# Two strips of squares moved from the end of the first projection to behind the second step of the second one

## The chip, the core and the metric

The kernel runs on one core of a Trainium2 chip. Each core has a matrix engine (TensorE, in the profile PE, its weight loads PEld), a vector engine (VectorE, DVE), an engine for activations, casts and copies (ScalarE, ACT), a general engine (GpSimd, POOL) and one that issues loads (SyncE, SP). Each runs its own queue of instructions in order, and semaphores join them. Transfers between memory and the core's buffers go over 16 DMA engines that all queues share; in this kernel SP's queue issues the loads and ACT's queue the stores. The metric is the time of one execution on the device in microseconds, as the median of several runs.

## The reference

The reference is one layer of a hybrid block over 1024 positions of width 1024, all in float32. Cut to what matters:

```python
proj = h @ w_in                                   # h: normed x with scale and shift from c
gm_u, gm_v, gm_z, ssm_z, xbc, dt_raw, g_a, g_b = jnp.split(proj, SPLITS, axis=-1)
y_a = spatial_gating(gelu(gm_u), gelu(gm_v), ...) * silu(gm_z)
...
y_b = ssd_scan(xh, dt, a, bm, cm) + xh * d_skip[:, None]
yz = (y_b.reshape(b, s, 2048) * silu(ssm_z)).reshape(b, s, 8, 256)
y_b = rms_norm(yz, ssm_norm_w.reshape(8, -1)).reshape(b, s, 2048)
merged = sigmoid(g_a) * (y_a @ w_proj_a) + sigmoid(g_b) * (y_b @ w_proj_b)
return rms_norm(x + gate * (merged @ w_out), final_norm_w)
```

The change concerns `rms_norm(yz, ...)`: in each of the 8 groups a position's 256 values are divided by the root of their mean square. The sum of squares over 256 values lies across partitions in the kernel, so it is made on TensorE.

## The kernel before

The kernel holds activations transposed: the channel on the 128 partitions, the position in the free dimension, in halves of 512. A large product is computed with each float32 operand as a high part (rounded, type fp32r) and a low part (the rest), and three matmuls: high x high, high x low, low x high.

**Stages.** Norm and modulation; the product with `w_in`; the gMLP branch; then the state-space branch, 8 groups of 4 heads each, two groups at a time. Beside this branch runs the *first projection* (`y_a @ w_proj_a`, function `proj_a`): 8 blocks of 24 pairs of matmuls (`pma`), which `draw(n)` issues n pairs at a time to fill TensorE. At a block's end VectorE forms `tha` from the block's two banks (L1488) and ACT's queue stores it as `mt_d` (L1490). Behind it comes the *second projection* (`y_b @ w_proj_b`), in Strassen's form: seven products of half size, p1, p3, p6, p5, p7, p2, p4 in this order, each of eight steps k. One step of one product is called a unit here: `multiply` (L1676), 12 matmuls, into four banks `x0p` to `x3p` or `y0p` to `y3p`. p1 uses the x banks; the y banks are first written by p3, at unit 8. After it come the product with `w_out` and the last norm.

**Operands of a unit.** `loads(u)` runs 6 units ahead (LOAD): it issues on SP's queue the load `yn` of the unit's 128 channels from `yb_d`, for every second such load the factors `rb` (L91, `rs_d` of the group, the same for all partitions), and the weight, either a strip `p1r` of 256 KB or a ready pair of high and low part (`p3a`, 512 KB, from `wb_d`). `operands(u)` runs 4 units ahead (LEAD): VectorE normalises `yn` with `rb` (L1614), ScalarE casts the high half `bh` (L1651), VectorE forms the low half `bl` (L1652); for p1 the same two steps for the weight (L1656, L1657). Units 0 to 7 (p1) need the normalised channels of groups 0 to 3, units 8 to 15 (p3) those of groups 4 to 7; the first unit that needs group 6 is unit 12, group 7's is unit 14.

**The factors of a group.** `post` stores a half (512 positions) of `yz` to `yb_d`; the squares follow (ScalarE, L1246 or L1251, then POOL adds the two tiles of a group, L1247). `post2` makes the sums: four small matmuls with a strip of ones, one for each 128 positions, into four 32-row strips of one bank. This is the *strip of squares*, in the profile `pq<-yz,ones`. VectorE scales the bank into a constant's tile that is free by then, `cwt` for an even group and `tri` for an odd one (L1267), and ACT's queue stores it as `ms_d` (L1268). `post3` loads that as `ssq` (SP's queue, L91), `root` takes the power -1/2 on POOL (L1282), `post4` stores `rs_d` (ACT's queue, L94). For the second halves of the last two groups, 6 and 7, these steps are placed by hand: both strips among the last pairs of the first projection, `post3` and `root` behind unit 1, `post4` behind unit 4.

**What sets the order.** `pin` keeps an instruction where the program has it on its engine; all matmuls and all loads are pinned, the scalings and `ms_d` stores of these two strips too. What is not pinned is placed by the language's scheduler. For their completion the transfers of SP's and of ACT's queue take eight counters in turn (`DMAHW0` to `DMAHW7` in the order below), so each issue waits until the transfer eight places back, on whichever of the two queues, has landed.

Of the kernel before, what the change touches and what calls it, by code (L numbers as in the profile page):

```python
# [35 lines left out]
def hybrid_kernel(  # L36
# [1255 lines left out]
    groups = [Group(g) for g in range(NG)]  # L1292
    rows_bank = [bank]
# [222 lines left out]
    def draw(n):  # L1516
        for _ in range(n):
            left[0] -= next(fill, 1) is None
# [48 lines left out]
    def banks(name, c):  # L1567
        return [psb.tile([P, 512], F32, name=f"{name}{j}", tag=f"b{c}{j}") for j in range(4)]
# [52 lines left out]
    def loads(u):  # L1621

        nm, k = units[u]
        if nm in fresh:
            n, h = fresh[nm]
            y_load(n + k, h)
        aops[u] = t = big(f"{nm}a{k}", F32R).rearrange("p (v c) -> p v c", v=2)
        if nm in WB:
            load(f32(t), wb_d[k][:, WB[nm]])
        else:  # L1630
            raws[u] = raw = gate_slot(f"{nm}r{k}") if nm == "p1" else slot_tile(f"{nm}r{k}")
            n = k if nm == "p1" else KT + k
            load(raw, w_proj_b[n * P : (n + 1) * P, 0:512])
# [35 lines left out]
    def multiply(u, ps):  # L1669
        nm, k = units[u]  # L1670
        first = nm in ("p1", "p5", "p2", "p3")
        a, (bh, bl) = aops.pop(u), bops.pop(u)
        for j in range(4):
            js = slice(j * P, (j + 1) * P)
            for n, (v, r) in enumerate(((0, bh), (0, bl), (1, bh))):
                pin(PE.matmul(ps[j], a[:, v, js], r, start=first and n + k == 0, stop=n == 2 and k == KT - 1,  # L1676
                              skip_group_check=not first))
# [89 lines left out]
    def ahead(u):  # L1767
        if u + LOAD < len(units):
            loads(u + LOAD)
        if u + LEAD < len(units):  # L1770
            operands(u + LEAD)

    draw(left[0] - 8)
    groups[6].post2(1, groups[6].late[:1])
    for u in range(LOAD):
        loads(u)
        if u > 1:
            operands(u - 2)
        if u == 3:
            draw(left[0] - 3)  # L1780
            groups[7].post2(1, groups[7].late[:1])
    draw(left[0] + 1)
    room.extend(tag for k in (KT - 2, KT - 1) for tag in ya_tags[k])
    for tags, _ in (war_r[0], wah_r[0], wal_r[0], tha_r):
# [10 lines left out]
    for u, (nm, k) in enumerate(units):  # L1795
        if k == 0:
            if nm == "p1":
                first = {t: psb.tile([P, 512], F32, name=f"{t}p", tag=f"b{t}") for t in ('x0', 'x1', 'x2', 'y3', 'y0', 'y1', 'y2', 'x3')}
                psx, psy = ([first[f"{v}{j}"] for j in range(4)] for v in "xy")
            elif nm in ("p5", "p2"):  # L1800
                psy = banks(f"y{nm}", "y")
            ps = psy if nm in ("p2", "p5", "p3") else psx
        multiply(u, ps)
        ahead(u)
        if nm == "p1" and k == 2:
            for tags, _ in (y1_r, ym_r):
                room.extend(tags)
        if nm == "p1" and k in (1, 4):
            for late in groups[NG - 2 :]:
                late.post4() if k == 4 else late.post3()  # L1810
            if k == 1:
                for late in groups[NG - 2 :]:
                    late.root()
        if nm == "p2" and k == 4:
            room.extend(rb_r[0])
        if k % 2 and nm in GATES:
            gate_load(GATES[nm][0] + k // 2, GATES[nm][1])
        if nm == "p4":
            for at, f, a in BESIDE:
                if at == k:  # L1820
                    f(*a)
        if nm in ("p7", "p2", "p4") and k % 2 == (nm != "p4"):
            merged(*more.pop(0))
        if k == KT - 1:
            for j in range(4):
                with tc.high_priority():
                    if nm in ("p1", "p3", "p5"):
                        t = slot_tile(f"{nm}_{j}")
                        A.copy(t, (psx if nm == "p1" else psy)[j])
                        sums[nm, j] = t  # L1830
                    if nm == "p6":
                        V.tensor_add(sums["p3", j], sums["p3", j], psx[j])
                    elif nm == "p5":
                        V.tensor_add(sums["p3", j], sums["p3", j], sums["p5", j])
                        more.append((j, 1, sums["p3", j], f"p3_{j}"))
                    elif nm == "p7":
                        V.tensor_add(sums["p5", j], sums["p5", j], psx[j])
                        more.append((4 + j, 1, sums["p5", j], f"p5_{j}"))
                    elif nm == "p2":
                        V.tensor_add(sums["p1", j], sums["p1", j], psy[j])  # L1840
                        more.append((j, 0, sums["p1", j], f"p1_{j}"))
                    elif nm == "p4":
                        merged(4 + j, 0, None, None)
# [179 lines left out]
```

## Time and profile before

| what | value |
| --- | --- |
| median of 3 runs | 1369.64 us (1369.30 to 1369.72) |
| profiled execution | 1367.94 us, its span 1366.0 us |
| granted clock of TensorE in it | 0.999 |
| TensorE busy | 1352.3 us (99% of the span) |
| VectorE busy | 1045.9 us (77%) |
| ScalarE busy | 799.2 us (59%) |
| POOL busy | 192.5 us (14%) |
| strip of the second half of group 6 on TensorE | at 1124.37 us |
| the same of group 7 | at 1128.17 us |
| first matmul of the second projection | at 1130.02 us |

Times in the profile are microseconds from the start of the span. A row of a timeline gives an instruction's start, its length, engine, line, operation, and in brackets how long the engine had been idle before it and which engine or transfer ended that. A row with xN stands for several instructions in a run.

### The profile page before, as it was taken

To read this page: it belongs to the slowest core of one execution; us is meant where nothing else is said; L and a number is where in the kernel's file an instruction comes from. 1 tells how busy PE (TensorE), PEld (TensorE's weight loads), DVE (VectorE), ACT (ScalarE), POOL (GpSimd) and SP (SyncE) were. 2 spreads that over 40 slices of the span, in tenths; PEclk is the share of its full clock that TensorE was granted. 3 is DMA by queue.
4 is the path that set the end of the run, shared out by engine and by line. 5 is a ranking of instruction groups with operands and counts; after the bars stand their busy time and mean duration, and the time that the engine had idled before them with its cause. 6 is when DMAs were issued, how large, how long until landed. Compare 5 with 4: busy or idle time off the path is not lost.

```text
span 1366.0 us, 20176 instructions
## 1 busy us (share of the span) xinstructions
PE 1352.3 (99%) x6943; PEld 1116.6 (82%) x6943; DVE 1045.9 (77%) x1716; ACT 799.2 (59%) x1447; POOL 192.5 (14%) x191
## 2 busy tenths in 40 slices
PE   8999999999999999999999999999999999999997
PEld 7688888888888888888888888888888887888886
DVE  4786876777778888697887797458888866859976
ACT  5763666666666656466566556486877834233443
POOL 1000000000000000000000000006798971000002
PEclk9999999999999999999999999999999999999999
DMA  9674444334344657877656675589889959988903
GB/s 286 181 244 135 142 124 120 104 117 124 108 139 139 181 181 230 252 230 241 211 180 189 219 247 167 166 282 314 305 299 307 309 201 320 325 268 322 382 37 124
DMA packets 249530, 288.65 MB, mean 211 GB/s; under 512 B 16812, under 2 KB 196436, under 8 KB 249428
## 3 DMA queue, kind: packets, MB, share of 16 engines
q1 hardware_dynamic: 174868, 203.80, 46.9%
q10 hardware_dynamic: 74560, 83.57, 17.9%
q8 instruction: 55, 0.90, 0.3%
q14 instruction: 47, 0.39, 0.1%
HBM read 199.82 MB, written 87.49 MB: 210 GB/s over the span
## 4 chain that ended last, share of the span: by engine, by line
PE 92%; DMA 3%; DVE 2%; ACT 1%; SPq 1%; issue 0%; POOL 0%; POOLq 0%; DVEq 0%; ACTq 0%
PE xz L565 6%; PE xcb L565 6%; PE xx L565 6%; PE pma L82 6%; PE xuz L565 6%; PE xg L565 6%; PE ox L1867 3%; PE ycb L565 3%; PE vx L954 3%; PE yp L1676 3%; PE yz L565 3%; PE yx L565 3%; PE yg L565 3%; PE yuz L565 3%; PE yi L82 2%; PE sp L82 2%
## 5 line engine op out<-in xcount | busy, mean ns | idle before, releaser
L1123 POOL TENSOR_SCALAR_AFFINE_SELECT dcy<-dcy 128x1024 f32<-128x1024 f32 x32 | 35.3, 1103 | 790.6 <-ACT ea L1119 786.9
L1131 ACT ACTIVATE dcy<-dcy,nacs 128x128 f32<-128x128 f32 x256 | 78.3, 389 | 2.7 <-POOL dcy L1123 2.1
L1147 DVE TENSOR_TENSOR dcy<-dcy,pc 128x1024 f32<-128x1024 f32 x32 | 39.0, 1218 | 8.0 <-PE pc L85 6.4
L1229 POOL TENSOR_TENSOR yz<-y,sl 128x512 f32<-128x512 f32 x32 | 44.4, 1387 | 2.5
L82 PE MATMUL pma<-yh,wah 128*128 128x512 f32 x128 | 43.1, 418 | 0.0
L82 PE MATMUL pma<-yh,wal 128*128 128x512 f32 x128 | 42.5, 413 | 0.0
L82 PE MATMUL pma<-yl,wah 128*128 128x512 f32 x128 | 40.2, 396 | 0.0
L1119 ACT ACTIVATE ea<-dcy 64x512 f32<-64x512 f32 x64 | 39.8, 622 | 0.7 <-DMA dcy<-acs_d 0.3
L1024 ACT ACTIVATE ac<-ac 128x1024 f32<-128x1024 f32 x32 | 33.9, 1061 | 10.2 <-DVE ac L1022 10.0
L1614 DVE SCALAR_TENSOR_TENSOR yn<-yn,par,rb 128x512 f32<-128x512 f32 x32 | 25.4, 793 | 18.6 <-DMA yn<-yb_d 16.9
L1154 ACT COPY bn<-pc 128x256 f32<-128x256 f32 x32 | 11.9, 371 | 46.9 <-DVE dcy L1147 46.9
L1228 POOL TENSOR_TENSOR y<-y,ym 128x512 f32<-128x512 f32 (+1 forms) x32 | 37.0, 1155 | 1.9 <-DVE ym L1226 1.9
L1022 DVE SCALAR_TENSOR_TENSOR ac<-c2x,cwt,ac 128x1023 f32<-128x1023 f32 (+2 forms) x24 | 30.7, 1279 | 6.1 <-ACT ac L1020 6.0
L82 PE MATMUL yi<-dcy,xd 128*64 128x128 f32 x512 | 35.0, 279 | 0.0
L1022 DVE SCALAR_TENSOR_TENSOR ac<-c2cb,cwt,ac 128x1023 f32<-128x1023 f32 (+2 forms) x24 | 30.6, 1274 | 5.6 <-ACT ac L1020 5.5
L1882 POOL TENSOR_TENSOR r<-r,fnw 128x512 f32<-128x512 f32 x4 | 5.3, 1344 | 204.8 <-ACT junk L1880 204.8
L986 ACT ACTIVATE vm<-vm,vr 128x128 f32<-128x128 f32 x64 | 25.8, 484 | 14.2 <-DMA vm<-v_d 13.7
L1226 DVE TENSOR_TENSOR ym<-yn,ea 128x512 f32<-128x512 f32 (+1 forms) x32 | 19.9, 622 | 18.5 <-PE yn L82 18.4
L824 ACT CAST wbb<-wbr 128x512 fp32r<-128x512 f32 x32 | 19.8, 619 | 22.8 <-DMA wb_d<-wbb 17.0
L82 PE MATMUL sp<-xe,bn 128*128 128x256 f32 x112 | 32.7, 409 | 0.0
L82 PEld LDWEIGHTS yn<-sl,st 128*128 128x128 f32 x224 | 29.7, 191 | 2.8 <-POOL st L1192 0.4
L82 PEld LDWEIGHTS yi<-dcy,xd 128*64 128x64 f32 x512 | 27.3, 136 | 5.7 <-issue 3.1
(2963 smaller groups left out, 4372.8 us busy)
## 6 DMA issues: line engine op xcount, KB each, us to landing
sl<-s_d SPq DMA_DIRECT2D x32, 768.0 KB, 6.4
s_d<-ac ACTq DMA_DIRECT2D x32, 512.0 KB, 3.3
wb_d<-wbb ACTq DMA_DIRECT2D x32, 512.0 KB, 3.4
dcy<-acs_d SPq DMA_DIRECT2D x32, 512.0 KB, 5.3
av<-in_w_in_dram SPq DMA_DIRECT2D x36, 256.0 KB, 2.9
aw<-in_ada_w_dram SPq DMA_DIRECT2D x16, 512.0 KB, 6.6
wbr<-in_w_proj_b_dram SPq DMA_DIRECT2D x32, 256.0 KB, 5.1
yb_d<-yz ACTq DMA_DIRECT2D x32, 256.0 KB, 6.0
```

What stands on the lines that cost most here:

```text
L82: pin(PE.matmul(acc, l, r, start=first, stop=last))
L565: pin(PE.matmul(ps, lw[:, k * P : (k + 1) * P], r[k], start=first and n + k == 0, stop=n == 2 and k == 3, skip_group_check=not first))
L954: pin(PE.matmul(ps[pn][j], l[:, j * P : (j + 1) * P], r, start=nm in ("p1", "p5", "p2") and n + units[i][1] == 0, stop=n == 2 and k == 3, ...
L1022: V.scalar_tensor_tensor(ac[:, s:], cc[:, : S - s], conv_wt[:, 3 - s, i : i + 1], ac[:, s:], op0=ALU.mult, op1=ALU.add)
L1119: link("A", lambda: A.activation(ea[hh * HD : (hh + 1) * HD], dcy.rearrange("p (j e) i l -> p e j (i l)", e=2)[hh * HD : (hh + 1) * HD, hh ...
L1123: link("G", lambda: G.affine_select(out=d8, in_=d8, compare_op=ALU.is_ge, fill=-1e30, base=0, pattern=[[0, 2 * HPG], [1, P]], channel_mult ...
L1131: link("A", lambda: A.activation(dcy[:, h, i, :], dcy[:, h, i, :], AF.Exp, bias=sub[:, i, h : h + 1]))
L1147: link("V", lambda: V.tensor_tensor(d3, d3, pc[:, 0:256].unsqueeze(1).to_broadcast([P, HPG, 256]), op=ALU.mult))
L1228: link("G", lambda: G.tensor_add(y1[:, :, t0:], y1[:, :, t0:], m[:, :, t0:]))
L1229: link("G", lambda: G.tensor_mul(yz, y1, sl[:, 4:6]))
L1676: pin(PE.matmul(ps[j], a[:, v, js], r, start=first and n + k == 0, stop=n == 2 and k == KT - 1, skip_group_check=not first))
L1867: pin(PE.matmul(ps, a[:, tsl], b[:, cs], start=first and n + j == 0, stop=n == 2 and j == 3, skip_group_check=not first))
```

## The change

Both strips of the second halves of groups 6 and 7, with their scalings and `ms_d` stores, are taken out of the end of the first projection. They are issued behind unit 1 of the second projection (p1, k = 1), and write the banks `y2p` and `y3p`, which p3 uses from unit 8 on. `post3` (the loads `ssq`) and `root` move from behind unit 1 to behind unit 2. `post4` stays behind unit 4. No instruction is added or removed.

```diff
     draw(left[0] - 8)
-    groups[6].post2(1, groups[6].late[:1])
     for u in range(LOAD):
         loads(u)
         if u > 1:
             operands(u - 2)
         if u == 3:
             draw(left[0] - 3)
-            groups[7].post2(1, groups[7].late[:1])
     draw(left[0] + 1)
...
-        if nm == "p1" and k in (1, 4):
+        if nm == "p1" and k in (1, 2, 4):
+            if k == 1:
+                rows_bank[0] = lambda name: psy[2 + ("pq6_1", "pq7_1").index(name)]
             for late in groups[NG - 2 :]:
-                late.post4() if k == 4 else late.post3()
-            if k == 1:
+                (None, lambda: late.post2(1, late.late[:1]), late.post3, None, late.post4)[k]()
+            if k == 2:
                 for late in groups[NG - 2 :]:
                     late.root()
```

**TensorE.** In the names below the part before a number is the tile's; `yh`, `yl`, `wah`, `wal` are high and low parts of the first projection's operands, `p1bh`, `p1bl`, `p1a` those of p1. The place is the last block of the first projection; - is before, + after:

```order
 L82 MATMUL pma_0_10857<-yh_8131,wah_1_10665 128x512
 L82 MATMUL pma_1_10860<-yh_8132,wah_1_10665 128x512
-L82 MATMUL pq_1_10913<-yz_2_10679,ones 32x128 x4
 L82 MATMUL pma_0_10857<-yl_8133,wah_1_10665 128x512
 L82 MATMUL pma_1_10860<-yl_8134,wah_1_10665 128x512
```

and, in the kernel after, the boundary between units 1 and 2:

```order
L1676 MATMUL x3p<-p1bh_10945,p1a_10922 128x512
L82 MATMUL y2p<-yz_2_10679,ones 32x128 x4
L82 MATMUL y3p<-yz_2_10749,ones 32x128 x4
L1676 MATMUL x0p<-p1bh_10969,p1a_10929 128x512
L1676 MATMUL x0p<-p1bl_10970,p1a_10929 128x512
```

Group 6's strip has gone from between two pairs of the last block (group 7's likewise, five pairs later), and both stand in a row between two units.

**SP's queue.** The loads around unit 8's, with the counters that each issue waits for. `rs_d_62` holds the factors of group 4, `yn_1` with `yb_d_99` and `p3a` with `wb_d_113` are unit 8's loads, `yb_d_100` is unit 9's, and `ms_d_72` and `ms_d_73` are the row sums of groups 6 and 7. Before:

```order
L91 DMA p1r_11064<-in_w_proj_b_dram 128x512 [waits DMAHW0_49]
L91 DMA ssq<-ms_d_72 128x8 [waits DMAHW1_49]
L91 DMA ssq<-ms_d_73 128x8 [waits DMAHW2_49]
L91 DMA rb_1_11089<-rs_d_62 128x512 [waits DMAHW3_49,DVE_49]
L91 DMA yn_1_11091<-yb_d_99 128x512 [waits DMAHW4_49]
L91 DMA p3a_11093<-wb_d_113 128x1024 [waits DMAHW5_49,PE_49,Pool_49]
L91 DMA yn_1_11114<-yb_d_100 128x512 [waits DMAHW6_49]
```

After:

```order
L91 DMA p1r_11050<-in_w_proj_b_dram 128x512 [waits DMAHW6_49]
L91 DMA rb_1_11083<-rs_d_62 128x512 [waits DMAHW7_49,DVE_49]
L91 DMA yn_1_11085<-yb_d_99 128x512 [waits DMAHW0_49]
L91 DMA p3a_11087<-wb_d_113 128x1024 [waits DMAHW1_49,PE_49,Pool_49]
L91 DMA ssq<-ms_d_72 128x8 [waits DMAHW4_49,DMAHW2_49]
L91 DMA ssq<-ms_d_73 128x8 [waits DMAHW5_49,DMAHW3_49]
L91 DMA yn_1_11112<-yb_d_100 128x512 [waits DMAHW6_49]
```

The two small loads `ssq` stood ahead of unit 8's three loads and stand behind them. In the kernel after, the counters `DMAHW0` and `DMAHW1` at `yn_1_11085` and `p3a_11087` are those of the two `mt_d` stores of the last block, and `DMAHW2` and `DMAHW3` at the `ssq` loads those of the two `ms_d` stores.

**ACT's queue.** Before, from the last square of group 7 on:

```order
L1246 ACTIVATE yz_2_10749<-yz_2_10749 128x512 x2
L1268 DMA ms_d_72<-cwt 4x128
L1651 CAST p1bh_10940<-yn_0_10922 128x512
L1656 CAST p1a_10924<-p1r_10925 128x512
L1651 CAST p1bh_10952<-yn_0_10927 128x512
L1656 CAST p1a_10929<-p1r_10930 128x512
L1656 CAST p1a_10979<-p1r_10980 128x512
L1268 DMA ms_d_73<-tri 4x128
L1651 CAST p1bh_10983<-yn_0_10934 128x512
```

After, from the stores of the last block's `tha` on to the casts for units 8 and 9 (`p3bh`):

```order
L1490 DMA mt_d_90<-tha_0_10855 128x512
L1490 DMA mt_d_90<-tha_1_10858 128x512
L1656 CAST p1a_11025<-p1r_11026 128x512
L1651 CAST p1bh_11053<-yn_0_10975 128x512
L1651 CAST p1bh_11090<-yn_0_11023 128x512
L1656 CAST p1a_11049<-p1r_11050 128x512
L1268 DMA ms_d_72<-cwt 4x128
L1268 DMA ms_d_73<-tri 4x128
L1651 CAST p1bh_11117<-yn_0_11047 128x512
L94 DMA rs_d_64<-ssq 128x8
L1651 CAST p3bh_11142<-yn_1_11085 128x512
L94 DMA rs_d_65<-ssq 128x8
```

The two `ms_d` stores have gone from ahead of and among the casts of p1's first units to behind the weight of unit 7 (`p1a_11049`), with the casts `p1bh` of units 6 and 7 before and behind them; `rs_d_64` and `rs_d_65`, the factors of groups 6 and 7, stand ahead of the casts of units 8 and 9. On VectorE the scalings `cwt` and `tri` have moved likewise, from among the normalisations of units 1 to 4 to behind that of unit 8, and the low half of unit u stands behind the normalisation of unit u + 1 or u + 2, one normalisation less ahead than before.

## Prediction

> **What bounds the kernel now.** I read the page first (busy time and the chain that ended last), then TensorE's waits from 1100 us to the end, and then each engine's timeline around the two strips and around the loads that follow them.
>
> ```profile
> span 1366.0 us, 20176 instructions
> PE 1352.3 (99%) x6943; PEld 1116.6 (82%) x6943; DVE 1045.9 (77%) x1716; ACT 799.2 (59%) x1447; POOL 192.5 (14%) x191
> PE 92%; DMA 3%; DVE 2%; ACT 1%; SPq 1%; issue 0%; POOL 0%; POOLq 0%; DVEq 0%; ACTq 0%
> ...
> PE pq L82 <- POOL yz L1247: 1.4, 2, 0.8
> PE oy L1867 <- DVE ma11h L1715: 0.3, 1, 0.3
> ```
>
> TensorE (PE) is busy for 99% of the span and holds 92% of the chain. So a microsecond taken from PE's row is a microsecond of the span, and any later stretch in which PE runs dry is a loss. The last two rows are all that PE waits for in the final 266 us: twice it stands still ahead of a strip (`pq`) until GpSimd (POOL) has added the squares of group 6 or 7. The change takes these two places away.
>
> The profiled execution took 1367.94 us, 1.9 more than its span; it lies 1.7 below the median of 1369.64. The differences below are worked out on its clock and added to the median.
>
> **The gain at the strips.** PE's timeline, with start, length and idle time before:
>
> ```profile
> 1115.54 0.62 PE L82 MATMUL pma<-yh,wah 128*128 128x512 f32 x2
> 1116.09 0.65 PE L82 MATMUL pq<-yz,ones 128*32 128x128 f32 x16
> 1116.66 0.74 PE L82 MATMUL pma<-yl,wah 128*128 128x512 f32 x2
> 1117.24 0.63 PE L82 MATMUL pma<-yh,wal 128*128 128x512 f32 x2
> ...
> 1123.18 0.61 PE L82 MATMUL pma<-yh,wah 128*128 128x512 f32 x2
> 1124.37 0.43 PE L82 MATMUL pq<-yz,ones 128*32 128x128 f32 x8 [0.57 <-POOL yz L1247]
> 1128.17 0.42 PE L82 MATMUL pq<-yz,ones 128*32 128x128 f32 x8 [0.84 <-POOL yz L1247]
> 1130.02 0.39 PE L1676 MATMUL x0p<-p1bh,p1a 128*128 128x512 f32 x1
> ...
> 1184.41 0.39 PE L1676 MATMUL x0p<-p6bh,p6a 128*128 128x512 f32 x1
> 1184.64 0.39 PE L1676 MATMUL x0p<-p6bl,p6a 128*128 128x512 f32 x1
> ```
>
> The last two rows give the step from one undisturbed matmul of this size to the next, 0.23, so a pair is 0.455 and twelve of them are 2.72. Nine pairs of `pma` remain from the one at 1123.18 on, itself included. Without the strips the second projection could start at 1123.18 + 9 x 0.455 = 1127.3 instead of 1130.02: 2.7 us, of which 1.4 is idle time. That is the upper bound of the gain, and it is just under 0.2% of the span.
>
> Two parts of it are lost again. First, the strips still run, now behind unit 1 (a unit is one step k of one product, 12 matmuls; unit 0 is p1's k = 0). Both strips of the first halves together stand between the pairs at 1115.54 and 1117.24: 1.70 less two pairs of 0.455 is 0.8. There they wait for nothing: POOL has the squares of group 7 ready at 1128.1, where the strip at 1128.17 starts. Second, unit 0 needs its operands:
>
> ```profile
> 1125.98 0.64 ACT L1246 ACTIVATE yz<-yz 128x512 f32<-128x512 f32 x1 [0.43 <-DMA yb_d<-yz]
> 1126.23 0.75 DVE L1614 SCALAR_TENSOR_TENSOR yn<-yn,par,rb 128x512 f32<-128x512 f32 x1 [1.07 <-DMA yn<-yb_d]
> 1127.52 1.14 DVE L1614 SCALAR_TENSOR_TENSOR yn<-yn,par,rb 128x512 f32<-128x512 f32 x1 [0.54 <-DMA yn<-yb_d]
> 1129.19 0.68 DVE L1657 TENSOR_TENSOR p1a<-p1r,p1a 128x512 fp32r<-128x512 f32 x1
> ```
>
> The weight's low half (1129.19, ready at 1129.87) is made before the change behind the normalisation of the fourth operand, which waits for its load until 1127.52. In the new order it stands behind the third (1126.23), and ScalarE's (ACT's) casts follow its last square at 1126.6: cast, 0.6, low half of the operand, 0.6, low half of the weight, 0.6, so ready at 1128.4. A start that would be 1127.3 loses some 0.7 to this. From unit 2 on the kernel is then 2.7 - 0.8 - 0.7 = 1.2 us ahead.
>
> **The cost: the round trip of the row sums starts later.** A strip's result goes PE, VectorE (DVE) scaling, store `ms_d` on ACT's queue, load `ssq` on SP's, POOL's power, store `rs_d` on ACT's queue, load `rb` on SP's, normalisation of units 12 to 15. DVE takes its instructions in order, and SP too. Before:
>
> ```profile
> 1116.59 0.92 ACTq L1490 DMA_DIRECT2D mt_d<-tha  x2
> 1120.57 0.32 SPq L91 DMA_DIRECT2D yn<-yb_d  x1
> 1131.85 0.48 ACTq L1268 DMA_DIRECT2D ms_d<-tri  x1
> 1135.25 3.97 SPq L91 DMA_DIRECT2D ssq<-ms_d  x2
> 1136.87 0.93 ACTq L1490 DMA_DIRECT2D mt_d<-tha  x2
> 1138.90 0.32 SPq L91 DMA_DIRECT2D ssq<-ms_d  x1
> 1138.03 2.12 POOL L1282 TENSOR_TENSOR ssq<-ssq,nhalf 128x8 f32<-128x8 f32 x1 [9.92 <-DMA ssq<-ms_d]
> 1140.50 2.77 POOL L1282 TENSOR_TENSOR ssq<-ssq,nhalf 128x8 f32<-128x8 f32 x1 [0.36 <-DMA ssq<-ms_d]
> 1140.51 0.34 ACTq L94 DMA_DIRECT2D rs_d<-ssq  x1
> 1140.02 0.43 SPq L91 DMA_DIRECT2D yn<-yb_d  x1
> 1144.27 0.75 DVE L1614 SCALAR_TENSOR_TENSOR yn<-yn,par,rb 128x512 f32<-128x512 f32 x1 [2.50 <-DMA yn<-yb_d]
> 1139.65 0.32 SPq L91 DMA_DIRECT2D rb<-rs_d  x1
> 1147.51 0.32 SPq L91 DMA_DIRECT2D rb<-rs_d  x1
> ```
>
> After the change the order puts the two scalings behind the normalisation of unit 8, both `ms_d` stores behind ACT's work for unit 7, and both `ssq` loads behind unit 8's loads on SP. Unit 8's `yn` load in its turn waits for the first `mt_d` store (the counter of the transfer eight places back). Step by step:
>
> - The low half of unit 0 starts at about 1127.2 (cast from 1126.6). Ten DVE instructions of 0.6 to 0.7 lead to `tha`, at 1133.4; its first half is stored from 1134.1.
> - How long that store takes is not fixed. It took 2.0 when SP stood still (1136.87, the load that waits for it goes at 1138.90) and 4.0 when loads were on the way (1116.59 to 1120.57). In the new place SP has not been stopped by `ssq` before, so I take 4.0: `yn` of unit 8 is issued at 1138.1.
> - From that issue to the normalisation 4.25 (1140.02 to 1144.27), and 0.75 for it: 1143.1. The scalings take 0.3, `ms_d` is issued at 1143.4.
> - `ms_d` to `ssq` took 3.4 (1131.85 to 1135.25): 1146.8. Everything behind it on SP waits till then, unit 9's `yn` first, which before went at 1140.96.
> - `ssq` to POOL took 1.6 with quiet queues (1138.90 to 1140.50), POOL to the issue of `rs_d` 2.5 (1138.03 to 1140.51): 1150.9.
> - `rs_d`, again 2.0 to 4.0 by the `mt_d` rows and up to 6.0, the median of the larger `yb_d` stores of the same queue (quoted below). Loads for units 9 to 11 go out together from 1146.8, so 4.0: the `rb` of units 12 and 13 is issued at 1154.9 instead of 1147.51.
> - `rb` to the normalisation that needs it 4.6 (1139.65 to 1144.27): 1159.5.
> - On ACT's queue the two `rs_d` stores stand ahead of the casts for units 8 and 9, so these wait for POOL too. Unit 8 lies 12 units ahead of unit 20 (1184.41), at 1151.8, or 1150.6 with the 1.2 won. Its cast can only run from 1151.2 (the store's 0.3 behind 1150.9); with 0.6 for it and 0.6 for the low half PE stops here first, by some 2 us. That isn't added to what follows: who is late by the larger amount further on has it in that.
>
> ```profile
> 1154.01 0.75 DVE L1614 SCALAR_TENSOR_TENSOR yn<-yn,par,rb 128x512 f32<-128x512 f32 x1 [1.25 <-DMA yn<-yb_d]
> 1163.33 0.75 DVE L1614 SCALAR_TENSOR_TENSOR yn<-yn,par,rb 128x512 f32<-128x512 f32 x1 [1.43 <-DMA yn<-yb_d]
> 1182.74 0.68 DVE L1652 TENSOR_TENSOR p6bl<-yn,p6bh 128x512 fp32r<-128x512 f32 x1
> ...
> core 0: us, PE busy (x) PEld busy (x) DVE busy (x) ACT busy (x) POOL busy (x), PEclk, DMA share, GB/s
> 1139.00:1142.00 3.00, 3.00 (x15) 2.49 (x14) 2.77 (x5) 1.12 (x2) 2.64 (x2) 1.00 0.43 77
> 1142.00:1164.00 22.00, 22.00 (x98) 18.21 (x97) 11.49 (x17) 7.33 (x13) 1.27 (x1) 1.00 1.03 387
> 1164.00:1181.00 17.00, 17.00 (x76) 14.08 (x75) 16.93 (x29) 5.06 (x9) 0.00 (x0) 1.00 1.04 401
> ...
> yb_d<-yz ACTq DMA_DIRECT2D x32, 256.0 KB, 6.0
> ```
>
> The normalisation at 1154.01 is unit 12's, so the operands come 5.5 us late. Before the change 1139 to 1142 is a hole in the transfers (share 0.43); from 1142 on the DMA engines are full (1.03, 1.04), so I take it that what is late at unit 12 is not made good: unit 16's normalisation at 1163.33 moves by the same 5.5. From there DVE has no gap (16.93 of 17.00) to the low half of unit 20, which ends at 1183.42, 1.2 ahead of the matmul that reads it (1184.64, above). The new order has 30 DVE instructions in this stretch instead of 32 (each low half stands behind one normalisation less), 1.2 us by rows of 0.6. So PE at unit 20 stands 5.5 - 1.2 - 1.2 = 3.1 us later than before, and the 1.2 won at the start are in that already. **The sum:** net = the delay less 2.4, and never under -1.2; with 5.5 it is +3.1, or 1372.7 for the median. The bounds: with every store at 2.0 the delay stays under 2.4 and the sum is -1.2; with `rs_d` at 6.0 the delay is 7.5 and the sum +5.1. Nothing behind unit 20 gives it back, since PE has no idle time there to fill. POOL's row and all other work is the same in number and order, at no cost.
>
> **The rivals.** (A) *The round trip stays hidden, not slower.* If a small store on ACT's queue always lands in the 2.0 of the quiet row, `yn` of unit 8 goes at 1136.1, `ms_d` at 1141.4, `ssq` at 1143.4, `rs_d` at 1147.5 and `rb` at 1149.5, 2.0 late: under the 2.4 at which it decides. The time is then 1369.64 - 1.2 = 1368.4. For it: the row at 1136.87. Against it: `ms_d` took 3.4 and loaded `mt_d` 4.0. The Trainium skill ("DMA: Bandwidth & Descriptors", section "Queues, rings and completion order") says that each DMA engine takes its queue rows in turn, packet by packet, so that a small store need not sit out the backlog of another queue; by it the sum would be this rival's. The 3.4 and 4.0 of this trace do not bear it out, but they do not exclude it for single stores; by these rows A has the chance given below.
>
> (B) *Half hidden.* One of `mt_d` and `rs_d` is quick (2.0) and the other takes 4.0: the delay is 3.5, the net +1.1, the time 1370.7. SP standing still ahead of `ssq` speaks for a quiet `rs_d`.
>
> (C) *Worse.* `rs_d` takes 6.0, as the bound above: +5.1, 1374.7. That the `rb` and `yn` rows of 1147.51 and 1154.01 lie 6.5 apart under full queues, and not 4.6, speaks for it; that SP stands still just before, against it.
>
> (D) *The strips wait in their new place too*, for banks or squares. The order shows no wait there but POOL's, which ended at 1128.1, some 4 us before; it would cost the 1.4 of idle time again, on top of A: 1369.8.
>
> **How the numbers follow.** The forecast (delay 4.8 to 6.5, 1372.0 to 1373.7) 0.45, A 0.16, B 0.22, C 0.15, D 0.02. About 0.2%, 2.7 us, is what a measurement of this kernel can tell from no change. Faster by more would need the whole upper bound: 0.03, out of A. Within it: the rest of A, B, D and the lower edge of the forecast (0.05), 0.42. Slower: 0.55. The range reaches from between A and B, 1369.1, to a little past C's price, 1375.2; what it leaves out is most of A (0.14) and the part of C in which more than one store is slow (0.05).
>
> **What would show it.** PE's two waits ahead of `pq` are gone, the two strips stand behind unit 1 without a wait, and p1 starts at about 1128. SP's `ssq` loads go near 1147 and the `rb` of unit 12 near 1155; there the transfers show a longer hole, 1140 to 1147, than before. DVE's normalisation of unit 16 starts near 1169, and PE gets idle time on the operands of p3 and p6 (`p3bh`, `p3bl`, `p6bl`), some 4 us in all up to unit 20. I am wrong if `rb` goes before 1150, or if PE shows no idle time between units 8 and 23.

## The result and the profile after

The changed kernel takes 1374.56 us (median of five runs, 1374.22 to 1376.06) against 1369.64 of the kernel before; the ratio is 1.0039, 95% interval 1.0027 to 1.0050. Measured once more beside three other kernels (e11 below) it is 1.0033, 1.0020 to 1.0045. So by the ratios it is slower by 4.5 to 5.3 us, inside the range, but above the forecast of 1372.7 and above the upper edge, 1373.7, that the prediction gave to it.

Single executions of one kernel differ by 3.5 us here (the kernel before beside the changed one, 1367.75 to 1371.20), by about 5 on two other chips and by 11 on a third, and some of it lies before the place of the change: the strip of the first halves (`pq`, sixteen matmuls), which the change doesn't touch, begins at 1116.09 in the first profile of the kernel before, at 1117.71 in that of the changed one. All comparisons of profiles below are therefore made from this strip on; a time of the changed kernel less 1.62 is a time on the clock of the prediction.

The first lines of the changed kernel's page and TensorE's waits from 1100 us on:

```profile
span 1373.3 us, 20171 instructions
PE 1354.7 (99%) x6943; PEld 1115.7 (81%) x6943; DVE 1045.1 (76%) x1716; ACT 799.1 (58%) x1447; POOL 191.6 (14%) x191
...
PE x0p L1676 <- DVE p6bl L1652: 2.3, 3, 1.3
PE y0p L1676 <- DVE p3bl L1652: 1.3, 2, 0.7
PE x0p L1676 <- DVE p1bl L1652: 1.0, 1, 1.0
PE oy L1867 <- DVE ma11h L1715: 0.3, 1, 0.3
```

The two waits ahead of `pq` are gone, and three others have come: for the low halves of p6, of p3 and, right at the start, of p1. TensorE's timeline at the start of the second projection, at the strips' new place, and at the beginning of unit 24 (p5):

```profile
1117.71 0.65 PE L82 MATMUL pq<-yz,ones 128*32 128x128 f32 x16
...
1129.08 0.49 PE L1676 MATMUL x0p<-p1bh,p1a 128*128 128x512 f32 x1
1130.59 0.50 PE L1676 MATMUL x0p<-p1bl,p1a 128*128 128x512 f32 x1 [1.01 <-DVE p1bl L1652]
...
1136.41 0.43 PE L82 MATMUL y2p<-yz,ones 128*32 128x128 f32 x8
1136.65 0.40 PE L82 MATMUL y3p<-yz,ones 128*32 128x128 f32 x8
1136.98 0.50 PE L1676 MATMUL x0p<-p1bh,p1a 128*128 128x512 f32 x1
...
1202.59 0.39 PE L1676 MATMUL yp<-p5bh,p5a 128*128 128x512 f32 x1
```

In the kernel before, the last of these stood at

```profile
1195.30 0.39 PE L1676 MATMUL yp<-p5bh,p5a 128*128 128x512 f32 x1
```

From the strip to unit 24 it is 84.88 us after and 79.21 before: 5.67 more, which is the whole loss between these two executions from the strip on. Behind unit 24 both kernels take the same.

The round trip in the changed kernel, in the order of its steps: ACT's stores, SP's loads, GpSimd's power, VectorE's normalisations of units 8, 12 and 16:

```profile
1136.71 0.92 ACTq L1490 DMA_DIRECT2D mt_d<-tha  x2
1141.69 0.32 SPq L91 DMA_DIRECT2D yn<-yb_d  x1
1144.37 0.75 DVE L1614 SCALAR_TENSOR_TENSOR yn<-yn,par,rb 128x512 f32<-128x512 f32 x1 [2.10 <-DMA yn<-yb_d]
1145.36 0.50 ACTq L1268 DMA_DIRECT2D ms_d<-cwt  x1
1146.95 0.90 SPq L91 DMA_DIRECT2D ssq<-ms_d  x2
1147.90 0.42 SPq L91 DMA_DIRECT2D yn<-yb_d  x1
1148.56 3.25 POOL L1282 TENSOR_TENSOR ssq<-ssq,nhalf 128x8 f32<-128x8 f32 x2 [18.58 <-DMA ssq<-ms_d]
1150.24 0.35 ACTq L94 DMA_DIRECT2D rs_d<-ssq  x1
1150.81 0.89 SPq L91 DMA_DIRECT2D p3a<-wb_d  x1
1157.34 0.32 SPq L91 DMA_DIRECT2D rb<-rs_d  x1
1162.30 0.75 DVE L1614 SCALAR_TENSOR_TENSOR yn<-yn,par,rb 128x512 f32<-128x512 f32 x1 [3.23 <-DMA yn<-yb_d]
1173.01 0.75 DVE L1614 SCALAR_TENSOR_TENSOR yn<-yn,par,rb 128x512 f32<-128x512 f32 x1 [2.09 <-DMA yn<-yb_d]
```

and what SP's queue waited for from 1134 to 1160 (in all, times, longest):

```profile
SPq L91 <- DMA mt_d<-tha: 6.0, 2, 5.7
SPq L91 <- DMA rs_d<-ssq: 5.6, 1, 5.6
SPq L91 <- DMA ms_d<-cwt: 4.2, 1, 4.2
```

Three stores of ACT's queue hold SP's queue for 15.8 us in turn: `mt_d` ahead of unit 8's `yn`, `ms_d` ahead of the first `ssq`, `rs_d` ahead of unit 12's `rb`. In the kernel before, such waits came to 5.1 us in the same stretch, and none for `rs_d` is listed:

```profile
SPq L91 <- DMA mt_d<-tha: 3.7, 2, 3.3
...
SPq L91 <- DMA ms_d<-tri: 1.4, 1, 1.4
```

The windows show the hole in the transfers that this makes: a share of 0.44 over 7 us, where the kernel before had one of 0.43 over 3 us (1139 to 1142) and 1.03 from there on:

```profile
core 0: us, PE busy (x) PEld busy (x) DVE busy (x) ACT busy (x) POOL busy (x), PEclk, DMA share, GB/s
1140.00:1147.00 7.00, 7.00 (x33) 5.79 (x32) 4.62 (x9) 1.82 (x4) 0.00 (x0) 1.00 0.44 145
1147.00:1158.00 11.00, 10.39 (x46) 8.28 (x45) 3.77 (x6) 2.02 (x4) 3.25 (x2) 1.00 0.80 236
```

### The profile page after: what moved, and what is told of

The parts are those of the page before. It is cut to its first block, busy times and chain, and to the rows that moved or that the text cites. A ratio compares the mean times of both kernels' runs of the same rounds, so it can differ in the third digit from the quotient of the medians.

```text
span 1373.3 us, 20171 instructions
## 1 busy us (share of the span) xinstructions
PE 1354.7 (99%) x6943; PEld 1115.7 (81%) x6943; DVE 1045.1 (76%) x1716; ACT 799.1 (58%) x1447; POOL 191.6 (14%) x191
## 4 chain that ended last, share of the span: by engine, by line
PE 87%; DMA 5%; DVE 4%; ACT 2%; SPq 1%; issue 1%; POOL 0%; POOLq 0%; DVEq 0%; ACTq 0%
PE xcb L565 6%; PE xz L565 6%; PE xx L565 6%; PE pma L82 6%; PE xuz L565 6%; PE xg L565 6%; PE ox L1867 3%; PE ycb L565 3%; PE vx L954 3%; PE yp L1676 3%; PE yz L565 3%; PE yx L565 3%; PE yuz L565 3%; PE yg L565 3%; PE yi L82 2%; PE sp L82 2%
```

## The experiments

Two questions stood after this. Which lateness sets the end: that of the factors of groups 6 and 7, that of the loads which stand behind `ssq` on SP's queue, or the strips' new place as such? And which half of the change makes it: the strips behind unit 1, or the row-sum loads behind unit 2? In each table row below "rb" and "unit 16" are the lateness of unit 12's `rb` issue and of unit 16's normalisation against the first profile of the kernel before (1147.51 and 1163.33), "unit 24" that of the first matmul of p5, all from the strip of the first halves on. These three columns are of one execution each. The profiled execution of the kernel before, which they are measured against, was 1.7 us below its median, that of e1 was 1.9 and that of e6 4.2 above theirs; partly for that, "unit 24" comes out 1.2 to 2.6 above what the ratio says in eight of the rows. What a kernel costs is read from the ratio; the columns are for the steps within an execution.

| kernel | ratio to before | 95% interval | rb | unit 16 | unit 24 |
| --- | --- | --- | --- | --- | --- |
| changed kernel | 1.0039 | 1.0027 to 1.0050 | 8.2 | 8.05 | 5.67 |
| e11, changed kernel again | 1.0033 | 1.0020 to 1.0045 | 8.3 | 7.20 | 4.83 |
| e1, row sums of groups 4 and 5 loaded | 1.0000 | 0.9991 to 1.0009 | 2.4 | 4.34 | 1.97 |
| e2, factors of group 5 loaded | 1.0012 | 1.0003 to 1.0021 | 2.6 | 5.52 | 3.15 |
| e3, row-sum loads on GpSimd's queue | 1.0047 | 1.0033 to 1.0060 | 8.2 | 8.64 | 6.35 |
| e4, row-sum loads behind unit 1 | 1.0013 | 1.0005 to 1.0022 | 3.4 | 3.47 | 1.26 |
| e10, both parts one unit earlier | 1.0000 | 0.9991 to 1.0009 | 4.2 | 4.74 | 1.90 |
| e12, changed kernel, `mt_d` later in turn | 1.0016 | 1.0007 to 1.0025 | 6.2 | 6.48 | 4.12 |
| e6, TensorE sums both tiles | 1.0026 | 1.0013 to 1.0039 | 8.5 | 8.60 | 6.20 |
| e5, kernel before again | one run | | 1.1 | 1.82 | 0.78 |
| e7, before, row-sum loads behind unit 2 | 1.0028 | 1.0017 to 1.0039 | 6.6 | 6.27 | 5.28 |
| e9, e7 with `mt_d` later in turn | 1.0003 | 0.9994 to 1.0012 | 2.9 | 2.72 | 1.59 |
| e8, version with the strips at the end | 0.9998 | 0.9986 to 1.0010 | 1.1 | 1.43 | 1.03 |

**e1: no wait for the moved strips.**

```diff
-            load(self.columns(), ms_d[self.g].rearrange("o (p c) -> (o p) c", p=P))
+            load(self.columns(), ms_d[self.g - 2 if self.g >= NG - 2 else self.g].rearrange("o (p c) -> (o p) c", p=P))
```

> The changed kernel, but the two loads of the row sums fetch those of groups 4 and 5, which lie in memory long before; so neither SP's queue nor the factors wait for the moved strips, and groups 6 and 7 are normalised with the wrong factors. Strips, scalings and stores stay where the change put them. Theory (the late round trip costs it all): the loss goes; what is left is the start of the second projection, where the profile shows no gain and no loss, so 1369.0 to 1370.2, ratio 0.9995 to 1.0005, and no idle time of TensorE between units 8 and 23. Rival (the strips' new place on TensorE, VectorE or ScalarE costs it): still 1374 to 1375.

Ratio 1.0000: the loss goes when the round trip no longer waits for the strips, though they stand where the change put them. TensorE still waits 0.9 for `p1bl` at the start, and in this profile 1.6 at p6, which I had not expected; that profile was of an execution 1.9 above the median. SP's queue still waits 5.6 for `mt_d` ahead of unit 8, and unit 12's `rb` is still 2.4 late. The strips' place on TensorE, VectorE and ScalarE as such does not cost the 5 us, and neither does unit 8's wait for `mt_d` by itself.

**e2: SP still stands ahead of the row-sum loads, but no load waits for the late factors.**

```diff
-            load(rb, rs_d[n // 2][:, hs].to_broadcast([P, 512]))
+            load(rb, rs_d[min(n // 2, NG - 3)][:, hs].to_broadcast([P, 512]))
```

> The changed kernel, but the factors of groups 6 and 7 (rb) are loaded from those of group 5; so SP still stands ahead of the two row-sum loads, but no load waits for the late factor stores (groups 6 and 7 get the wrong factors). If the late factors alone cost it: all is won back, 1369.0 to 1370.2. If SP's standing still ahead of the row-sum loads alone costs it: 1374 to 1375. By the profile both have a part: the normalisations of units 10 and 11, which need no late factor, are 4.7 us late, unit 16's 8.1; with 4.7 left at unit 16 the rule 'delay less 2.4' gives +2.3, 1371.9, and I expect 1371 to 1372.5.

Ratio 1.0012, 1.6 us: a third of the loss stays. Of the two ends that a single cause would have given, 1374 to 1375 (1.0032 and more) is excluded, and 1370.2 (1.0004) lies just inside the interval, at its lower edge. The two causes lie one behind the other: SP's standing still brings units 9 to 11 late, the wait for `rs_d` adds to that.

**e3: the row-sum loads on GpSimd's queue.**

```diff
-            load(self.columns(), ms_d[self.g].rearrange("o (p c) -> (o p) c", p=P))
+            src = ms_d[self.g].rearrange("o (p c) -> (o p) c", p=P)
+            if self.g < NG - 2:
+                load(self.columns(), src)
+            else:
+                pin(G.dma_start(self.columns(), src))
```

> The changed kernel, but the two row-sum loads go over GpSimd's queue, so that SP's queue does not stand ahead of them; the factors of groups 6 and 7 still come late. If SP's standing still alone costs it: 1369.0 to 1370.5. If the late factors alone cost it: 1374 or a little more, since the factors come no earlier. By both parts: units 9 to 11 come some 3 us earlier and their loads do not queue ahead of the factor stores in one burst; rb of unit 12 at 1154 to 1157 in the clock of the changed kernel's profile (1157.3 there), delay 5 to 6.5 at unit 16, +2.6 to +4, 1372.2 to 1373.7.

Ratio 1.0047, no better than the changed kernel. My sum of both parts, up to 1373.7 or 1.0030, was wrong: it lies below the interval, and unit 12's `rb` is as late as in the changed kernel (8.2). SP's queue runs on, and stops for longer at the next place. What it waits for from 1132 to 1160, the two stores ahead of GpSimd's loads, and those loads:

```profile
SPq L91 <- DMA rs_d<-ssq: 10.0, 1, 10.0
SPq L91 <- DMA mt_d<-tha: 5.9, 2, 5.6
...
1146.48 0.50 ACTq L1268 DMA_DIRECT2D ms_d<-cwt  x1
1147.08 0.48 ACTq L1268 DMA_DIRECT2D ms_d<-tri  x1
...
1153.26 1.30 POOL L1281 DMA_DIRECT2D ssq<-ms_d  x2 [22.38 <-DMA yn<-yb_d]
```

With SP's loads let through, the small store `ms_d` now shares the engines with them: 6.8 us pass from its issue to the load that needs it, with a DMA share of 1.03 meanwhile, where the changed kernel's took 1.6 (1145.36 to 1146.95) at a share of 0.08. The view puts the end of GpSimd's wait down to a load `yn`, but the store is late by itself: the trace has the last count of its completion at 1152.68, 6.2 us after the issue. What was won by not stopping is paid back by the store.

**e4: only the strips moved.** The row-sum loads and the power stay behind unit 1.

```diff
-        if nm == "p1" and k in (1, 2, 4):
+        if nm == "p1" and k in (1, 4):
...
+                for late in groups[NG - 2 :]:
+                    late.post2(1, late.late[:1])
...
-                (None, lambda: late.post2(1, late.late[:1]), late.post3, None, late.post4)[k]()
-            if k == 2:
+                late.post4() if k == 4 else late.post3()
+            if k == 1:
```

> The changed kernel, but the row-sum loads and the power stay behind unit 1, where they were before the change: on SP's queue they stand ahead of unit 8's loads again, and the scalings on VectorE no longer behind unit 8's normalisation. The strips stay in their new place. Row-sum stores 1138 instead of 1145.4 in the clock of the changed kernel's profile, row-sum loads near 1142, rb of unit 12 near 1152 (1157.3 in the changed kernel). Theory (delay of that rb less 2.4): delay 2.5 to 4, +0.1 to +1.6, 1369.7 to 1371.2. Rival (the strips' place): 1374 to 1375. Rival (SP's standing still, whose length here is as before or longer, 6 us against 5): no better than 1373.

Ratio 1.0013, 1.8 us, a little above the expected 1371.2 in ratio terms. The row-sum stores came at 1141.8 on the changed kernel's clock (1143.32 here), earlier than its 1145.4 but not at the expected 1138. SP now stops for long only once, for the strips' own result, ahead of unit 8's loads:

```profile
SPq L91 <- DMA ms_d<-cwt: 8.3, 1, 8.3
...
SPq L91 <- DMA rs_d<-ssq: 0.9, 1, 0.9
```

So SP standing still for 8.3 us in one piece costs less than 15.8 in three, and the strips' half of the change is worth a third of the loss.

**e5: the kernel before, unchanged.**

> The kernel before, unchanged, for a second profile. It is to tell how far two executions of the same kernel lie apart from the strip of the first halves (1116.09 us in the first profile) on. If the rule 'end = lateness of unit 16's normalisation less 2.4' is to carry, the distance from that strip to unit 24 must come out as before within a few tenths (79.2 us). If it is 1 to 2 us longer, differences of that size between single profiles, as e1's +2.0 against a measured ratio of 1.0000, say nothing.

It came out 0.78 longer, with unit 16's normalisation 1.82 late. So one profile tells differences of 2 us poorly, and small ones are read from the ratios.

**e6: TensorE sums both tiles, GpSimd adds nothing.**

```diff
-            G.tensor_add(sq[0], sq[0], sq[1])
...
-                mm(pq[32 * i : 32 * i + 32, 0:P], ones[:, 0:32], sq[0][:, i * P : (i + 1) * P])
+                for j, s in enumerate(sq):
+                    mm(pq[32 * i : 32 * i + 32, 0:P], ones[:, 0:32], s[:, i * P : (i + 1) * P], j == 0, j == len(sq) - 1)
...
```

> The changed kernel, but GpSimd does not add the squares of the last two second halves; TensorE sums both tiles (eight small matmuls a strip instead of four, about 0.6 us more). Theory for the start: unit 0's low half took 1.77 instead of 0.68 because GpSimd's addition ran beside it; so it takes 0.7 here, TensorE's wait of 1.0 for p1bl goes, and p3 starts 0.3 to 0.5 earlier than in the changed kernel against the strip of the first halves. Theory for the end: the end hangs on the round trip alone, which starts 1.1 earlier: 1.0 to 1.2 below the changed kernel, ratio to before 1.0025 to 1.0035. If GpSimd has nothing to do with the 1.77, it stays. If the start's wait counts for the end by itself, beside the round trip: ratio 1.0018 or lower.

The first low half of p1 and what ran beside it; VectorE and GpSimd of the changed kernel:

```profile
1128.77 1.77 DVE L1652 TENSOR_TENSOR p1bl<-yn,p1bh 128x512 fp32r<-128x512 f32 x1
1130.46 0.68 DVE L1657 TENSOR_TENSOR p1a<-p1r,p1a 128x512 fp32r<-128x512 f32 x1
...
1128.14 1.84 POOL L1247 TENSOR_TENSOR yz<-yz 128x512 f32<-128x512 f32 x1 [2.21 <-ACT yz L1246]
```

and VectorE in e6:

```profile
1129.91 0.68 DVE L1652 TENSOR_TENSOR p1bl<-yn,p1bh 128x512 fp32r<-128x512 f32 x1
```

The low half takes 0.68 without the addition and 1.77 beside it, and TensorE's wait for `p1bl` is gone. p3 starts 1.0 earlier than in the changed kernel against the strip, more than the 0.3 to 0.5 expected. The Trainium skill ("SBUF — State Buffer", section "Who interferes with whom") says that a VectorE instruction with two inputs in SBUF contends with a GpSimd instruction that reads SBUF; these rows agree. Whether the end follows can't be told: the ratio, 1.0026, is in the expected 1.0025 to 1.0035, but its interval holds the changed kernel's 1.0033 and 1.0039 as well. In the profile, of an execution 4.2 above the median, the loss at unit 24 is no smaller (6.20). That the round trip would come 1.1 earlier did not show there: against the strip `mt_d` is stored 0.9 earlier than in the changed kernel (1137.36 less 3.17 here), `ms_d` only 0.1 (1146.79 less 3.17). What ate the rest was not tried.

**e7: only the row-sum loads moved.** The kernel before with

```diff
-        if nm == "p1" and k in (1, 4):
+        if nm == "p1" and k in (2, 4):
...
-            if k == 1:
+            if k == 2:
```

> The kernel before with one part of the change alone: the row-sum loads and the power stand behind unit 2, the strips stay in the first projection. On SP's queue the row-sum loads then stand behind unit 8's loads, as in the changed kernel, but their data are there by 1135. Theory (it is the lateness of the row sums that costs, not their place on SP's queue): ratio 0.9995 to 1.0007, no idle time of TensorE ahead of p3. Rival (the place on SP's queue costs it): 1.002 or more.

Here my theory fell. The row sums are in memory as early as before the change, and the ratio is 1.0028, 3.8 us slower. SP's waits, the load `ssq` and `rb` of unit 12:

```profile
SPq L91 <- DMA rs_d<-ssq: 5.6, 1, 5.6
...
SPq L91 <- DMA mt_d<-tha: 4.7, 2, 4.4
...
SPq L91 <- DMA ms_d<-tri: 1.6, 1, 1.6
...
1133.45 0.48 ACTq L1268 DMA_DIRECT2D ms_d<-tri  x1
...
1142.90 0.90 SPq L91 DMA_DIRECT2D ssq<-ms_d  x2
1155.32 0.32 SPq L91 DMA_DIRECT2D rb<-rs_d  x1
```

The row sums are stored from 1133.45 and loaded at 1142.90: the loads stand behind unit 8's `yn`, and that waits for the `mt_d` store, which has nothing to do with it but for the counter that both use. The new theory: the gate is this wait.

**e8: a version meant to beat both.** e6's sum on TensorE in the kernel before, with both strips behind the last pair of the first projection:

```diff
-    groups[6].post2(1, groups[6].late[:1])
...
-            draw(left[0] - 3)
-            groups[7].post2(1, groups[7].late[:1])
+            draw(left[0])
+            for g in groups[NG - 2 :]:
+                g.post2(1, g.late)
...
```

> A version meant to beat both: TensorE sums both tiles as in e6, and both strips stand behind the last pair of the first projection, ahead of unit 0, where TensorE would wait for unit 0's operands anyway; row-sum loads and power behind unit 1 and the stores of the factors behind unit 4 as before the change. Theory: no wait for GpSimd, the strips of 1.2 in all fill part of the wait for the operands, and the round trip starts no later than 1131 as before: unit 2 starts 1.0 to 1.5 earlier against the strip of the first halves, the lateness of unit 16's normalisation stays under 2.4: 0.5 to 1.5 us faster, ratio 0.9989 to 0.9997. Rival (the round trip is later than that because the first strip's scaling comes 6 us later than before): same or slower, 1.0000 to 1.0015.

Ratio 0.9998, 0.9986 to 1.0010: no difference that can be told. The two waits at the strips go and unit 2 starts 1.4 earlier against the strip, as expected; but TensorE waits 1.6 for a low half of p1 at unit 6 instead.

**e9: e7 without the gate.** The two `mt_d` stores of the last block stand behind unit 2 in the program; by that they take their counters after unit 8's loads.

```diff
-            for h in range(2):
-                keep(nc.scalar.dma_start(mt_d[dd][:, h * 512 : (h + 1) * 512], ths[h]))
+            if dd < KT - 1:
...
+            else:
+                last_th.extend(ths)
...
+            if k == 2:
+                for h in range(2):
+                    pin(nc.scalar.dma_start(mt_d[KT - 1][:, h * 512 : (h + 1) * 512], last_th[h]))
```

> e7 with the two stores mt_d of the last block placed in the program behind unit 2, so that in the counters' turn they come after unit 8's loads and no load ahead of the row-sum loads waits for them. Theory (e7 loses because the row-sum loads stand behind unit 8's loads, and these wait for the mt_d stores through the counters): unit 8's yn is issued some 4 us earlier than in e7 (1141.8 there), the row-sum loads near 1139 instead of 1142.9, rb of unit 12 near 1151.5 instead of 1155.3, all in e7's clock; delay at unit 16 2 to 3 instead of 6.3, ratio 1.0005 to 1.0015. Rival (standing behind unit 8's loads costs it through the transfers alone, or unit 2 comes too late by itself): the row-sum loads no earlier, ratio 1.0025 or more.

Ratio 1.0003, 0.9994 to 1.0012: the loss of e7 is gone. The stores still run when they did; only who waits for them has changed:

```profile
1135.82 0.90 SPq L91 DMA_DIRECT2D ssq<-ms_d  x2
1136.90 0.92 ACTq L1816 DMA_DIRECT2D mt_d<-tha  x2
1150.06 0.32 SPq L91 DMA_DIRECT2D rb<-rs_d  x1
```

`ssq` is loaded ahead of the `mt_d` stores, 5.5 us earlier than in e7 against the strip (7.1 less the 1.56 by which this run was early), and `rb` 3.7 earlier. The new theory holds for e7: without the gate its loss is gone.

The gate alone is not the whole of it, though. In e1 unit 8's `yn` stands behind the `mt_d` store too, and the sums lie in memory as in e7; yet e1 loses nothing that can be told. What differs most in the rows between is how fast `rs_d` lands: 2.6 us to unit 12's `rb` in e1, 6.3 in e7 (1149.03 to 1155.32). In e1:

```profile
1151.06 0.32 ACTq L94 DMA_DIRECT2D rs_d<-ssq  x1
...
1153.69 0.37 SPq L91 DMA_DIRECT2D rb<-rs_d  x1
```

Seven loads had left between `ssq` and this store in e7, four in e1, where SP was held up by the late `ms_d` stores meanwhile. No run changes this alone.

**e10: both parts one unit earlier.**

```diff
-        if nm == "p1" and k in (1, 2, 4):
-            if k == 1:
+        if nm == "p1" and k in (0, 1, 4):
+            if k == 0:
...
-            if k == 2:
+            if k == 1:
```

> The changed kernel with both halves of the change one unit earlier: strips behind unit 0, row-sum loads and power behind unit 1 (ahead of unit 8's loads on SP). Against e4 (strips behind unit 1, the same otherwise) the stores ms_d stand one cast earlier on ScalarE's queue. Theory (delay less 2.4): row-sum stores 1 to 2 us earlier than e4's against the strip of the first halves, delay 1.5 to 2.5 instead of 3.5, ratio 1.0000 to 1.0008. Rival (any place behind unit 0 costs as much as e4's): 1.0013.

Ratio 1.0000, 0.9991 to 1.0009: strips in the y banks cost nothing that can be told if they and the loads stand one unit earlier. But it also gains nothing, and it did not come about as I had thought: against the strip the row-sum stores come 0.9 later than e4's (1140.93 less 1115.99, against 1143.32 less 1119.23), not 1 to 2 earlier, and unit 16 is 4.7 late instead of 1.5 to 2.5. Why it costs less than e4 stays open.

**e11: the changed kernel again.**

> The changed kernel unchanged, beside e9, e10 and e12 on one chip: ratio 1.0027 to 1.0050 as measured before, delay at unit 16 of 7 to 9 and a loss at unit 24 of the delay less 2.4. If the delay is 2 us off from the first profile's 8.1 and the loss at unit 24 does not follow it, the rule falls.

Ratio 1.0033. Delay 7.20, loss 4.83: as the rule has it.

**e12: the changed kernel without the gate.** e9's edit in the changed kernel.

> The changed kernel with the mt_d stores out of the counters' turn as in e9. Theory: unit 8's yn is issued 2 to 4 us earlier than in the changed kernel, and with it its normalisation, the scalings behind it on VectorE, the row sums' stores and loads and rb of unit 12: delay 5 to 6 instead of 8.1, ratio 1.0018 to 1.0028. Rival (the wait through the counters is not what holds the round trip there): as the changed kernel, 1.0035 or more.

Ratio 1.0016 against 1.0033 for e11 on the same chip: about half of the loss goes, though the two intervals still touch (1.0007 to 1.0025, 1.0020 to 1.0045). SP's waits have no `mt_d` any more:

```profile
SPq L91 <- DMA rs_d<-ssq: 5.7, 1, 5.7
SPq L91 <- DMA ms_d<-cwt: 4.8, 1, 4.8
```

Unit 8's `yn` is issued 7.3 us earlier against the strip than in the changed kernel (1133.40 less 1116.70, against 1141.69 less 1117.71), the row sums are stored only 2.2 earlier (1142.19 less 1116.70, against 1145.36 less 1117.71), and unit 16 is 6.5 late instead of the expected 5 to 6. I take what is left for the strips' own lateness, since e4's 1.0013 is near; that is argued, not shown.

## Why the prediction came out as it did

The direction and the range held, and so did the path: the late round trip, through `mt_d`, `ms_d` and `rs_d`, sets the end. The size was 1.8 us short (+3.1 forecast, +4.9 by the medians). The steps of the round trip missed by more than the total shows. Up to unit 16's normalisation some 7 us were added (`tha` 1.0, `mt_d` 1.0, `rs_d` 3.1, `rb` to the normalisation 0.4, units 12 to 16 1.4), and some 4 saved (`yn` of unit 8 to its normalisation 1.6, `ms_d` 1.8, the power 0.8). That the time still fell in the range, near the price of rival C, is in part luck.

- **TensorE's waits at the strips go; the strips cost 0.8.** They went; the strips cost 0.57 (1136.41 to 1136.98).
- **1.2 us ahead from unit 2 on.** This step failed. Against the strip of the first halves p3 starts 0.08 later than before, not 1.2 earlier. The first matmul stood at 1127.46 on the old clock, but "low half of the operand, 0.6" took 1.77, since GpSimd's addition for group 7 ran beside it, and the weight's low half was ready at 1129.5 instead of 1128.4. The kernel before shows the same thing, in a row that I had quoted (a normalisation of 1.14 at 1127.52) without asking why it took 1.14. By the net rule below the end is set by the round trip, so that this term counts there only by the 1.0 by which `tha` came later.
- **`tha` stored from 1134.1, `yn` of unit 8 at 1138.1.** On the old clock 1135.1 and 1140.1: the 1.0 of the last point, and a store of 5.0 where I had taken 4.0.
- **`ms_d` 1143.4, `ssq` 1146.8, `rs_d` 1150.9.** Measured 1143.7, 1145.3 and 1148.6. The first agrees by luck: `yn` came 2.0 late, and from its issue to the normalisation it took 2.7 (1141.69 to 1144.37) where I had taken 4.25. `ms_d` took 1.6 instead of 3.4; SP had stood still by then, and the DMA share was 0.08 from 1145.4 to 1147. GpSimd's power took 1.7 to the issue of `rs_d` (1148.56 to 1150.24) instead of 2.5.
- **`rs_d` lands in 4.0, `rb` at 1154.9.** Mis-sized: 7.1 (1150.24 to 1157.34), over my upper bound of 6.0; `rb` at 1155.7. Seven loads leave from 1147.90 to 1150.81 when `ssq` lets SP go, and the 4 KB store that is issued among them lands only when most of theirs is through: by the completion counts in the trace it lands at 1157.28, behind the five loads issued ahead of it (the last at 1157.02) and ahead of the two issued after it (1157.69 and 1158.91). I had named these loads and still taken a value from a lighter stretch. The Trainium skill ("DMA: Bandwidth & Descriptors", section "Queues, rings and completion order"), which I had weighed for its turn-taking between queues, says in the same section that a completion is signalled only after the DMA engine's earlier writes, of all its queues; 7.1 us agrees with that sentence, and 1.6 in the silent stretch too.
- **Late by 5.5 at unit 12 and the same at unit 16.** 6.7 and 8.05. That the delay is not made good was right; that it doesn't grow was not. It grew by 0.7 each at units 14 and 16, which wait for their loads there; why was not tried.
- **Net = delay less 2.4.** This held, within an execution, in all seven profiles in which VectorE has as many instructions as in the changed kernel from unit 16's normalisation to the low half of unit 20 (30, where the kernel before has 32): 8.05 and 5.67, 7.20 and 4.83, 6.48 and 4.12, 4.34 and 1.97, 5.52 and 3.15, 8.64 and 6.35, 8.60 and 6.20. The shorter order was worth 1.4 us (18.70 against 20.09 from the one to the other), not 1.2, the room ahead of the matmul 1.2. In the kernels with 32 the room alone is left: 1.82 and 0.78, 6.27 and 5.28. The rest have other numbers, 29 in e4, 29 in e10, 31 in e9, 33 in e8: 3.47 and 1.26, 4.74 and 1.90, 2.72 and 1.59, 1.43 and 1.03. Where one of these comes near the rule, that says nothing for it.
- **The cause of the delay.** I laid it on the scalings behind unit 8's normalisation, and with them on the strips. The chain was right, its shares were not. The strips alone (e4) cost 1.8 us, the row-sum loads alone (e7) 3.8, with the sums in memory all the while; together 5.6, about the 4.5 to 5.3 of the changed kernel. With the row-sum loads behind unit 8's, the `mt_d` store stands in front of them through the counter (e9, e12); what that costs depends on how loaded `rs_d` then is (e1 against e7), and this last part is not shown by a run of its own.
- **The rivals.** A (hidden) would have needed every store at 2.0; the three took 5.0, 1.6 and 7.1. C, the slow `rs_d`, priced at +5.1 and given 0.15, is what happened, with the smaller delay before it; the forecast's own 4.0 for this store, with 0.45, did not. That the `rs_d` stores would stop TensorE at unit 8 did not come: unit 8's low half was ready 1.4 ahead, since the first `rs_d` was issued 2.3 earlier than forecast and unit 8 itself came no earlier than before; the first stop is at unit 9, for SP's late `yn`.

## What to carry to other kernels

Where transfers take completion counters in turn, a load waits for whatever took its counter last, here the transfer eight places back on either of the two queues: before a small load is moved past another on its queue, look up whose landing that other waits for. When a chain of small stores and loads feeds operands some units ahead, count its lateness at the last point where an engine has no gaps left, and compare it with the room ahead of the matmul there; TensorE's own waits at the change tell little. And take a small store's time from a stretch with the same load on the engines, not from the median of its name.

## What the runs showed of the hardware

A store of 4 KB or less took between 1.6 us (1145.36 to 1146.95, DMA share 0.08) and 7.1 us (1150.24 to 1157.34, seven loads issued around it) from its issue to the load that waited for it, in the same execution. The first of these, a 2 KB store, took 6.8 us in e3 (1146.48 to 1153.26) at a share of 1.03.

A VectorE subtraction of two 128x512 inputs took 0.68 alone and 1.77 beside a GpSimd addition, which itself took 1.84 there; with no such addition (e6) it took 0.68 at the same place. In the kernel before, a normalisation of 1.14 us, elsewhere 0.75, overlapped such an addition of 1.35, elsewhere 1.28. In the changed kernel this was worth 1.0 us, at a place where TensorE had nothing else to do.
